# Stick-breaking attention on one core: moving a group's first exponential, the read-outs and the restored halves

## The chip, the core and the metric

The kernel runs on one core of a Trainium2 chip. The core has five engines that run their own instruction streams and meet at semaphores: TensorE (PE, with its weight loads shown apart as PEld), VectorE (DVE), ScalarE (ACT), GpSimd (POOL) and SyncE (SP), which here only issues DMAs. The metric is the device time of one execution in microseconds. The kernel before took 1867.29 us (median of three runs, 1866.61 to 1867.33).

## The reference, cut to what matters

Two decoder layers on 512 tokens of width 2048. The first is an indexer-sparse attention layer and isn't touched. The second is stick-breaking attention over shared keys and values, 16 query heads in 4 groups, each with one key and value head:

```python
def mixer_b(x, w_in, w_o, k, v):
    q, gate = jnp.split(x @ w_in, [WIDTH_B], axis=-1)
    ...
        z = jnp.einsum('bqngd,bsnd->bngqs', qg, k).astype(jnp.float32) * (HEAD_DIM ** -0.5)
        strict = key_pos[None, :] < t[:, None]
        log_om = jnp.where(strict, -jax.nn.softplus(z), 0.0)
        suffix = lax.cumsum(log_om, axis=log_om.ndim - 1, reverse=True) - log_om
        a = jnp.where(strict, jnp.exp(jax.nn.log_sigmoid(z) + suffix), 0.0)
        o = jnp.einsum('bngqs,bsnd->bqngd', a.astype(v.dtype), v)
    ...
    return (o * jax.nn.silu(gate)) @ w_o
```

Everything is in float32. The kernel reaches that precision by splitting each operand into a high part and the rest (`split`: ACT copies the high part, DVE subtracts) and multiplying three times (`mm3`).

## The kernel before, in words

Activations are kept transposed: a block is 128 features by 512 tokens, `XH[k]` and `XL[k]` are the high and low part of block k of the layer's input, k from 0 to 15. The change lies in one stretch of the program, the stick-breaking layer's attention, from the first logits to the output projection.

**Groups and units.** The stretch runs four groups, g = 0 to 3, of four heads each. In a group, PE works on two things in turns. One is the gate projection: 16 blocks of weights by 4 banks, 64 steps of three 512-column matmuls (`gate(n)` issues n steps; names `g`, `xh`, `xl`, `wh`, `wl`). The other is ten units, `Sticks.units`, each one a pair of query block i and key block kb, four heads by 128 queries wide. Units 0, 1, 5 and 8 are on the diagonal and get a mask. A unit passes these stages:

- `logits`: three matmuls into a PSUM bank `z` (unit 0 in bank 7, the others by turns in 4 and 5); on the diagonal DVE adds the mask.
- `soft` and `plus`: three ACT operations (Abs, Exp, Ln) and one DVE operation make the softplus.
- `high` and `low`: DVE adds the running total, casts the high part `sh` and subtracts the low part `sl`; for kb > 0 ACT copies the rows that carry the total out of z into `t`.
- `weights`: two matmuls with a triangle add the suffix sums onto the same bank z, ACT takes the exponential, and for kb > 0 DVE subtracts z from `t`. Only then is the bank free for the unit after next.
- `halves`: ACT and DVE split the result into two `c` tiles.
- `values`: three matmuls into a bank `o` (6 or 7). The third one multiplies the low half.
- `leave`: for kb = 0, ACT reads the finished bank o out into F (`f<-o`).

**Turns.** `turn(s, gaps)` for s = 1 to 11 holds the logits and softplus of unit s, the weights and halves of unit s - 1 and the values of unit s - 2, with gate steps between them (`gaps`, from `TURNS`: 54 steps in all). A turn is called late when unit s is on the diagonal. On PE, ACT and DVE the order of the instructions in this stretch is written out by hand: `strictly` issues each one after the one before on its engine. So an instruction that waits holds up whatever stands behind it on the same engine. GpSimd is called directly, without that order.

**Weights of the gate.** `feed(most, ahead)` pushes as many gate items as will be needed within `ahead` gate steps; each item is one ACT copy (`wh<-raw`) and one DVE subtraction (`wl<-raw,wh`) into three rotating buffers. The raw weights come by DMA of 512 KB into three `raw` buffers, in the order of the list `units`. `others(n)` takes n pieces off a background list `bg`, in which queries and keys of the next group and the restored halves wait.

**Restored halves.** The Strassen products before this stretch have overwritten the right half (256 columns) of blocks 0 to 7. They are read back from a scratch tensor `x2` in DRAM, four blocks with each of two 512 KB units, and `restore` splits them into XH and XL again. Group 0 takes the gate's blocks in the order 8 to 15, 0 to 7 (`gate_first`), so block 0 is needed from gate step 32.

**Start and end of a group.** Group 0 runs 11 gate steps before its first turn, the others 10. `first_soft` takes units 0 and 1 through soft, plus, high and low. At the end the gate's 64 steps are filled up, the next group's two logits follow, then `close` applies the SiLU of the gate banks, and the table of ACT is switched.

Of the kernel before, what the change touches and what calls it, by code (L numbers as in the profile page):

```python
# [10 lines left out]
F32 = mybir.dt.float32  # L11
# [3 lines left out]
ALU = mybir.AluOpType  # L15
# [3 lines left out]
T = 512  # L19
H = T // 2  # L20
D = 2048
NK = D // 128
# [55 lines left out]
def trunk_kernel(  # L78
# [48 lines left out]
    act, dve, pool = (Paced(e) for e in (nc.scalar, nc.vector, nc.gpsimd))  # L127
    pool = nc.gpsimd
# [11 lines left out]
    def split(hi, lo, src, eng=dve):  # L140
        act.activation(hi, src, AF.Copy)
        eng.tensor_tensor(lo, src, hi.bitcast(F32), ALU.subtract)
# [12 lines left out]
    XH = [top.tile([128, T], F32R, name=f"xh{k}") for k in range(NK)]  # L155
    XL = [top.tile([128, T], F32R, name=f"xl{k}") for k in range(NK)]
# [16 lines left out]
    units = []  # L173
# [14 lines left out]
    def next_raw():  # L188
        while sent[0] < len(units) and len(raws) < 3:
            raw = top.tile([128, 2, 512], F32, name="raw", tag="raw", bufs=3)  # L190
            unit = units[sent[0]]
            if len(unit) == 1:
                _, k, n = unit[0].shape
            else:
                k, n = 2, unit[-1]
            raw = raw.rearrange("p a n -> p (a n)")[:, : k * n].rearrange("p (k n) -> p k n", k=k)
            if len(unit) == 1:
                nc.sync.dma_start(raw, unit[0])
            else:
                src, a, b, c0, n = unit  # L200
                rows = src.rearrange("(k p) n -> p k n", p=128)
                step = b - a
                if sent[0] < 2:

                    for i, cut in enumerate(((0, H if sent[0] else NSEL, T), (0, T))):
                        for lo, hi in zip(cut, cut[1:]):
                            halves.append((raw[:, i, lo:hi], rows[:, a + i * step, c0 + lo : c0 + hi]))
                    if len(halves) == 6:
                        for n in (1, 3, 4, 2, 5, 0):
                            nc.sync.dma_start(*halves[n])  # L210
                else:
                    nc.sync.dma_start(raw, rows[:, a : b + 1 : step, c0 : c0 + n])
            raws.append(raw)
            sent[0] += 1
        return raws.popleft()
# [38 lines left out]
    def weight_parts():  # L254
        return tuple(top.tile([128, 512], F32R, name=n, tag=n, bufs=3) for n in ("wh", "wl"))

    def plain_items(jobs):
        for n, nk in jobs:
            if n <= 128:
                for k in range(0, nk, 4):  # L260
                    if k % 8 == 0:
                        raw = next_raw()
                    parts = weight_parts()
                    four = [w[:, : 4 * n].rearrange("p (k n) -> p k n", k=4) for w in parts]
                    split(*four, raw[:, k % 8 : k % 8 + 4])
                    yield from zip(*([w[:, a] for a in range(4)] for w in four))
                continue
            for _ in range(nk // 2):
                raw = next_raw()
                for a in range(2):  # L270
                    wh, wl = weight_parts()
                    split(wh[:, :n], wl[:, :n], raw[:, a])
                    yield wh, wl
# [81 lines left out]
    def strictly(fn, *args):  # L355
        was, pinned[0] = pinned[0], 2
        fn(*args)
        pinned[0] = was
# [212 lines left out]
    for g in range(4):  # L571
        add_job(w_in_b, g * 512, strassen=True)
    x2 = dram.tile([D, T], F32, name="x2")
    for k in (4, 5, 6, None, 7, 0, None, 1, 2, 3):
        if k is None:
            first = 4 * (units[-1][1] == 0)
            units.append((x2.rearrange("(k p) t -> p k t", p=128)[:, first : first + 4, H:T],))
        else:
            units.append((w_in_b, 2 * k, 2 * k + 1, D, 512))
# [69 lines left out]
    late = slice(NSEL, T)  # L649
# [526 lines left out]


    def restore(raw, k):
        split(XH[k][:, H:T], XL[k][:, H:T], raw[:, k % 4])

    def gate_items():
        for k, n in ((0, 6), (4, 4)):
            yield from plain_items([(512, n)])
            raw = next_raw()
            bg.extend(lambda raw=raw, k=k: restore(raw, k) for k in range(k, k + 4))
            if k:
                bg.append(lambda: split_keys(1))
        yield from plain_items([(512, 6), *[(512, NK)] * 3])

    C3.extend(c3_tiles(pc_.enter_context(tc.tile_pool(name="pc1", bufs=1))))  # L1190
    V, K = ([tuple(spots[n : n + 2]) for n in where] for where in ((0, 2, 4, 6), (8, 14) * 2))
# [2 lines left out]
    def split_keys(g):  # L1194
        split(*K[g], Kf[:, g])
# [4 lines left out]
    def split_scaled(g, i):  # L1200
        qh, ql = (q.rearrange("p (h q) -> p h q", h=4) for q in Q[i])
        src = F[g][:, :, i * 128 : (i + 1) * 128]
        act.activation(qh, src, AF.Copy, scale=HSCALE)
        dve.scalar_tensor_tensor(ql, src, HSCALE, qh.bitcast(F32), ALU.mult, ALU.subtract)
# [63 lines left out]
    class Sticks:  # L1268
# [3 lines left out]
        units = [(3, 3), (1, 1), (3, 2), (1, 0), (3, 1), (2, 2), (3, 0), (2, 1), (0, 0), (2, 0)]  # L1272
# [97 lines left out]
        def turn(self, s, gaps):  # L1370

            late = self.diagonal(s)
            new = 1 < s < 10
            if new:
                strictly(self.logits, s)
                if late:
                    strictly(self.low, s - 1)
                strictly(self.soft, s)
                if not late:
                    strictly(self.plus, s)  # L1380
                    feed(1)
            gate(gaps[0])
            if s > 1:
                strictly(self.values, s - 2)
            gate(gaps[1])
            if s < 11:
                strictly(self.weights, s - 1)
                if new and late:
                    strictly(self.plus, s)
                strictly(self.halves, s - 1)  # L1390
                if new:
                    strictly(self.high, s)
                    if not self.diagonal(s + 1):
                        strictly(self.low, s)
            else:
                strictly(act.preload_act_table_set, "silu_and_others")
            if s > 1:
                strictly(self.leave, s - 2)

            if self.g < 3:  # L1400
                bg.extend(lambda i=i: split_scaled(self.g + 1, i) for i in {8 if self.g == 0 else 6: (1,), 9: (3,), 10: (0,)}.get(s, ()))
            if new and late:
                feed(1)
            else:
                feed()
                others(1 if self.g else 2)
            gate(gaps[2])
# [3 lines left out]
    def gate(n):  # L1411
        steps(gemm, n)
        gated[0] += n

    def feed(most=9, ahead=10):

        while most and items.count < min(64, -(-(gated[0] + ahead) // 4)):
            strictly(items.push)
            most -= 1
# [2 lines left out]
        for _ in range(min(n, len(bg))):  # L1422
            strictly(bg.popleft())

    def first_soft(u, ahead=18):
        strictly(sticks.soft, u)
        strictly(sticks.plus, u)
        feed(1, ahead)
        strictly(sticks.high, u)
        strictly(sticks.low, u)  # L1430

    LOG_EXP = "natural_log_exp_and_others"
    tc.keep_in_program_order(act.preload_act_table_set(LOG_EXP))
# [3 lines left out]
    sticks = Sticks(0)  # L1437
    strictly(sticks.logits, 0)
    for u, n in enumerate((6, 5)):
        for _ in range(n):  # L1440
            gate(1)
            if not u:
                feed()
        if not u:
            strictly(sticks.logits, 1)
            first_soft(0)
            first_soft(1, 14)
    bg.append(lambda: split_scaled(0, 0))

    TURNS = ((0, 0, 3), *[(1, 1, 3)] * 3, (2, 1, 3), *[(1, 1, 3)] * 2, (2, 1, 3), (1, 1, 3), (1, 1, 2), (1, 1, 3))  # L1450
    for g in range(4):
        for s in range(1, 12):
            if g and s == 2:
                bg.append(lambda g=g: split_scaled(g, 2))
            if 0 < g < 3 and s == 3:
                bg.append(lambda g=g: split_keys(g + 1))
            sticks.turn(s, TURNS[s - 1])
        gate(64 * (g + 1) - gated[0])
        others(len(bg))
        if g < 3:  # L1460
            then = Sticks(g + 1)
            for u in range(2):
                strictly(then.logits, u)

        def close(h):
            sg = work()
            act.activation(sg, banks[h], AF.Silu)
            dve.tensor_tensor(F[g][:, h], F[g][:, h], sg, ALU.mult)

        for h in range(4):  # L1470
            strictly(close, h)
        if g < 3:
            sticks = then
            feed(1)
            strictly(act.preload_act_table_set, LOG_EXP)
            for u in range(2):
                first_soft(u)
            banks = mm_banks("g")
            gemm = gemm_w(items, plain, banks)
            gate(10)  # L1480
    pk_.close()
    pc_.close()

# [55 lines left out]
```

## Time and profile before

| what | value |
| --- | --- |
| median of three runs | 1867.29 us |
| profiled execution: device time | 1867.0 us |
| profiled execution: span, first to last instruction | 1865.3 us |
| granted TensorE clock, mean | 0.999 |
| PE busy / PEld busy | 99% / 84% of the span |
| DVE, ACT, POOL busy | 66%, 50%, under 1% |

In the rows, PE is the matmul and PEld the load of its stationary operand. A matmul's duration includes the pipeline behind it: 512-column matmuls are listed with 389 ns, though on an undisturbed stretch they start every 0.227 us. So a busy share of 99% doesn't mean that PE runs at its peak; lost time shows as a larger distance between two starts. The names are those of the program with their numbers left out: `x` in a DMA row is `x2`. L116 and L118 are lines of the helpers that issue ACT's and DVE's instructions, so instructions are told apart by their tiles.

### The profile page before, as it was taken

To read this page: it belongs to the slowest core of one execution; us is meant where nothing else is said; L and a number is where in the kernel's file an instruction comes from. 1 tells how busy PE (TensorE), PEld (TensorE's weight loads), DVE (VectorE), ACT (ScalarE), POOL (GpSimd) and SP (SyncE) were. 2 spreads that over 40 slices of the span, in tenths; PEclk is the share of its full clock that TensorE was granted. 3 is DMA by queue.
4 is the path that set the end of the run, shared out by engine and by line. 5 is a ranking of instruction groups with operands and counts; after the bars stand their busy time and mean duration, and the time that the engine had idled before them with its cause. 6 is when DMAs were issued, how large, how long until landed. Compare 5 with 4: busy or idle time off the path is not lost.

```text
span 1865.3 us, 24806 instructions
## 1 busy us (share of the span) xinstructions
PE 1855.9 (99%) x9181; PEld 1575.5 (84%) x9181; DVE 1231.2 (66%) x2395; ACT 939.0 (50%) x1696; POOL 4.7 (0%) x20
## 2 busy tenths in 40 slices
PE   9999999999999999999999999999999999999998
PEld 8898888888888888888888999987787888888887
DVE  5668678566556444676467788887878745567534
ACT  3546333355555432475245444478888743347422
POOL 0000000000000000000000000000000000000000
PEclk9999999999999999999999999999999999999999
DMA  6442333322221432433334333332122253243333
GB/s 198 128 116 66 98 95 97 96 68 69 68 69 57 158 120 78 125 97 106 126 118 127 110 93 109 107 90 81 57 69 78 69 187 95 76 128 97 118 102 113
DMA packets 111178, 189.21 MB, mean 101 GB/s; under 512 B 8528, under 2 KB 29008, under 8 KB 111056
## 3 DMA queue, kind: packets, MB, share of 16 engines
q1 hardware_dynamic: 111056, 187.62, 33.2%
q8 instruction: 72, 1.18, 0.3%
q14 instruction: 50, 0.41, 0.1%
HBM read 179.21 MB, written 8.39 MB: 101 GB/s over the span
## 4 chain that ended last, share of the span: by engine, by line
PE 93%; ACT 3%; DVE 2%; issue 1%; DMA 0%; SPq 0%; DVEq 0%; ACTq 0%
PE g L145 11%; PE g L147 11%; PE g L146 11%; PE o L147 7%; PE o L146 7%; PE o L145 7%; PE m L145 4%; PE m L147 4%; PE m L146 4%; PE q L145 3%; PE q L147 3%; PE q L146 3%; ACT wk L116 2%; PE k L146 2%; PE k L147 2%; PE k L145 2%
## 5 line engine op out<-in xcount | busy, mean ns | idle before, releaser
L118 ACT ACTIVATE wh<-raw 128x512 fp32r<-128x512 f32 (+2 forms) x624 | 359.5, 577 | 687.2 <-PE g L146 220.3
L118 DVE TENSOR_TENSOR wl<-raw,wh 128x512 fp32r<-128x512 f32 (+2 forms) x623 | 387.6, 623 | 438.2 <-ACT wh L118 423.4
L145 PE MATMUL g<-xh,wh 128*128 128x512 f32 x1024 | 403.6, 394 | 0.0
L147 PE MATMUL g<-xh,wl 128*128 128x512 f32 x1024 | 399.7, 390 | 0.2 <-DVE wl L116 0.2
L146 PE MATMUL g<-xl,wh 128*128 128x512 f32 x1024 | 399.3, 390 | 0.0
L147 PEld LDWEIGHTS g<-xh,wl 128*128 128x128 f32 x1024 | 192.2, 188 | 42.0 <-DVE wl L116 1.0
L146 PEld LDWEIGHTS g<-xl,wh 128*128 128x128 f32 x1024 | 192.5, 188 | 37.1
L145 PEld LDWEIGHTS g<-xh,wh 128*128 128x128 f32 x1024 | 192.4, 188 | 37.0
L147 PE MATMUL o<-xh,wl 128*128 128x512 f32 x512 | 199.3, 389 | 0.0
L145 PE MATMUL o<-xh,wh 128*128 128x512 f32 x512 | 199.2, 389 | 0.0
L146 PE MATMUL o<-xl,wh 128*128 128x512 f32 x512 | 199.2, 389 | 0.0
L147 PEld LDWEIGHTS o<-xh,wl 128*128 128x128 f32 x512 | 96.1, 188 | 20.4 <-DVE wl L118 0.4
L145 PEld LDWEIGHTS o<-xh,wh 128*128 128x128 f32 x512 | 96.1, 188 | 20.0
L146 PEld LDWEIGHTS o<-xl,wh 128*128 128x128 f32 x512 | 96.1, 188 | 19.9
L145 PE MATMUL q<-xh,wh 128*128 128x512 f32 x256 | 99.6, 389 | 0.0
L146 PE MATMUL q<-xl,wh 128*128 128x512 f32 x256 | 99.6, 389 | 0.0
L147 PE MATMUL q<-xh,wl 128*128 128x512 f32 x256 | 99.6, 389 | 0.0
L118 ACT ACTIVATE sh<-st 128x512 fp32r<-128x512 f32 x80 | 49.7, 624 | 44.2 <-DVE st L118 44.1
L116 ACT ACTIVATE wk<-z 128x512 f32<-128x512 f32 x80 | 47.6, 595 | 36.1 <-DVE z L116 14.6
L118 DVE TENSOR_TENSOR sl<-st,sh 128x512 fp32r<-128x512 f32 x80 | 55.1, 690 | 13.9 <-ACT sh L118 13.9
L118 DVE TENSOR_TENSOR xl<-f,xh 128x512 fp32r<-128x512 f32 x80 | 54.3, 686 | 12.5 <-ACT f L118 12.3
L147 PEld LDWEIGHTS q<-xh,wl 128*128 128x128 f32 x256 | 48.0, 188 | 10.1
(298 smaller groups left out, 3396.7 us busy)
## 6 DMA issues: line engine op xcount, KB each, us to landing
raw<-w_in_a SPq DMA_DIRECT2D x95, 512.0 KB, 3.7
raw<-w_in_b SPq DMA_DIRECT2D x64, 512.0 KB, 3.8
raw<-w_ple_gate SPq DMA_DIRECT2D x52, 512.0 KB, 3.7
raw<-w_o_a SPq DMA_DIRECT2D x24, 512.0 KB, 3.8
raw<-w_o_b SPq DMA_DIRECT2D x24, 512.0 KB, 3.7
raw<-w_kv_b SPq DMA_DIRECT2D x16, 512.0 KB, 3.8
raw<-w_ple_gate SPq DMA_DIRECT2D x24, 256.0 KB, 2.9
f<-xT SPq DMA_DIRECT2D x4, 1024.0 KB, 6.4
```

The source lines that it names most:

```text
L116: ins = method(*args, **kw)
L118: ins = method(*args, **kw)
L145: pe.matmul(out, a[0], b[0], start=start, stop=False)
L146: pe.matmul(out, a[0], b[1], start=False, stop=False)
L147: pe.matmul(out, a[1], b[0], start=False, stop=stop)
```

## The change

Four things are changed, all in that stretch.

1. `first_soft` becomes `first_two`: unit 0 goes through soft, plus, one gate item, high and low as before, unit 1 only through soft and plus. Its high and low move into turn 1, behind the exponential and the halves of unit 0 and behind one gate item. Turn 1 takes no background piece any more.
2. The gate runs 11 steps ahead of turn 1 in groups 1 to 3 too. The count at the end of a group stays 64, so one step fewer stands at the end.
3. In late turns the gate item is pushed ahead of `high` in place of behind the read-out. The read-outs of units 3 and 6 move from turns 5 and 8, which are late, to the ends of turns 6 and 9; those of units 8 and 9 stay.
4. `restore` no longer uses ACT: DVE copies the high half and GpSimd subtracts. The second 512 KB of x2 is loaded one unit earlier, ahead of the weights of blocks 0 and 1, which take its later place.

```diff
-    for k in (4, 5, 6, None, 7, 0, None, 1, 2, 3):
+    for k in (4, 5, 6, None, 7, None, 0, 1, 2, 3):
         if k is None:
-            first = 4 * (units[-1][1] == 0)
+            first = 4 * (units[-1][1] == 14)
             units.append((x2.rearrange("(k p) t -> p k t", p=128)[:, first : first + 4, H:T],))
...
     def restore(raw, k):
-        split(XH[k][:, H:T], XL[k][:, H:T], raw[:, k % 4])
+        hi, lo = XH[k][:, H:T], XL[k][:, H:T]
+        dve.tensor_copy(hi, raw[:, k % 4])
+        pool.tensor_tensor(lo, raw[:, k % 4], hi.bitcast(F32), ALU.subtract)
...
-        for k, n in ((0, 6), (4, 4)):
+        for k, n in ((0, 6), (4, 2)):
...
-        yield from plain_items([(512, 6), *[(512, NK)] * 3])
+        yield from plain_items([(512, 8), *[(512, NK)] * 3])
...
                 strictly(self.halves, s - 1)
-                if new:
+                if late or s == 1:
+                    feed(1)
+                if s < 10:
                     strictly(self.high, s)
                     if not self.diagonal(s + 1):
                         strictly(self.low, s)
             else:
                 strictly(act.preload_act_table_set, "silu_and_others")
-            if s > 1:
-                strictly(self.leave, s - 2)
...
-            if new and late:
-                feed(1)
-            else:
+            if not late:
+                for u in {6: (3,), 9: (6,), 10: (8,), 11: (9,)}.get(s, ()):
+                    strictly(self.leave, u)
                 feed()
                 others(1 if self.g else 2)
...
-    def first_soft(u, ahead=18):
-        strictly(sticks.soft, u)
-        strictly(sticks.plus, u)
-        feed(1, ahead)
-        strictly(sticks.high, u)
-        strictly(sticks.low, u)
+    def first_two():
+        for u in range(2):
+            strictly(sticks.soft, u)
+            strictly(sticks.plus, u)
+            if not u:
+                feed(1, 18)
+                strictly(sticks.high, u)
+                strictly(sticks.low, u)
...
-            first_soft(0)
-            first_soft(1, 14)
+            first_two()
...
-            for u in range(2):
-                first_soft(u)
+            first_two()
...
-            gate(10)
+            gate(11)
```

## The prediction

> **What bounds the kernel now.** I read the engines' busy times first, then the four groups as windows, each from its first logits to the next group's, and then the matmuls of an undisturbed stretch (name, count, duration, first and last start).
>
> ```profile
> PE 1855.9 (99%) x9181; PEld 1575.5 (84%) x9181; DVE 1231.2 (66%) x2395; ACT 939.0 (50%) x1696; POOL 4.7 (0%) x20
> ```
>
> ```profile
> 1234.03:1299.02 64.99, 63.91 (x275) 50.15 (x273) 53.14 (x91) 50.30 (x90) 1.24 (x6) 1.00 0.28 81
> 1299.02:1362.26 63.24, 62.65 (x272) 50.85 (x273) 49.73 (x82) 51.98 (x89) 0.00 (x0) 1.00 0.23 67
> 1362.26:1424.99 62.73, 62.27 (x273) 50.82 (x272) 49.89 (x82) 51.50 (x88) 0.00 (x0) 1.00 0.23 68
> 1424.99:1488.96 63.97, 63.08 (x273) 50.66 (x272) 49.92 (x81) 51.64 (x88) 0.00 (x0) 1.00 0.21 66
> ```
>
> ```profile
> L145 PE MATMUL o<-xh,wh x83: 389/389/389, 1489.0 to 1544.7; 128*128 128x512 f32 x83
> ```
>
> PE is the bound, and no matmul is removed. Undisturbed, 82 triples start in 55.7 us: 0.2264 us a matmul. A group is 64 x 3 + 10 x 8 = 272 matmuls, so 61.6 us. The four windows are longer by 3.4, 1.6, 1.1 and 2.4 us. These 8.5 us are all that the change can win, 0.45% of the time, and less than it can lose. So the question is which waits of PE go and which come. The list of PE's waits (total, times, longest) names the largest:
>
> ```profile
> PE o L1362 <- DVE c L116: 1.1, 3, 0.5
> PE z L145 <- DVE t L116: 1.0, 4, 0.4
> PE z L145 <- ACT f L116: 0.5, 1, 0.5
> ```
>
> It counts only time in which the modelled pipeline is empty. Starts in the timeline (start, duration) tell more:
>
> ```profile
> 1311.63 0.39 PE L1361 MATMUL o<-c,c 128*128 128x512 f32 x1
> 1312.39 0.50 PE L1362 MATMUL o<-c,c 128*128 128x512 f32 x1 [0.37 <-DVE c L116]
> 1312.73 0.39 PE L145 MATMUL g<-xh,wh 128*128 128x512 f32 x1
> ```
>
> The two distances, 0.76 and 0.34, exceed 0.227 by 0.53 and 0.11: 0.64 us where 0.37 is listed. I add 0.27 to each listed wait.
>
> **The change part by part.** *(a) The first exponential.* The wait above is unit 0's third values matmul, in group 1. Its way through ACT, and the start on DVE:
>
> ```profile
> 1307.21 1.30 ACT L116 ACTIVATE wk<-wk 128x512 f32<-128x512 f32 x2
> 1308.41 0.62 ACT L116 ACTIVATE wh<-raw 128x512 fp32r<-128x512 f32 x1
> 1309.26 0.59 ACT L116 ACTIVATE t<-z 32x512 f32<-32x512 f32 x1 [0.23 <-DVE wk L116]
> 1309.88 0.60 ACT L116 ACTIVATE wk<-z 128x512 f32<-128x512 f32 x1
> ...
> 1308.54 0.69 DVE L116 SCALAR_TENSOR_TENSOR wk<-z,wk 128x512 f32<-128x512 f32 x1 [0.95 <-ACT wk L116]
> ```
>
> The exponential (1309.88) stands behind unit 1's gate item and total. Moved up it starts at 1308.5, 1.4 us sooner, and the low half behind it comes at about 1311.0 in place of 1312.34. PE wants it at 1311.63 + 0.23 = 1311.86. All three waits of that kind go: 1.1 + 3 x 0.27 = 1.9 us. Late next is unit 1: its cast and low part now follow, on DVE, the softplus of 1308.54, the total, the half and a gate item. At 0.6 us each (steps between starts, as on ACT) that is 1308.54 + 4 x 0.6 + 0.45 + 0.69 = 1312.1; its weights want it one values matmul, one gate step and one matmul after 1311.86, at 1313.0. Margin 0.9 us. Small waits beside these, at the weights and values of the first units, I put at -0.3 (bounds 0 and -1).
>
> *(b) Eleven steps.* In groups 1 to 3 the step taken from the end stands at the start, so between unit 9's weights and the next unit 0's there are as many steps as before; only the logits in between come 0.68 us (three matmuls) sooner. Unit 0's bank is 7, which unit 9's read-out frees:
>
> ```profile
> 1359.80 1.28 ACT L116 ACT_TABLE_LOAD   x1
> 1361.10 0.60 ACT L116 ACTIVATE f<-o 128x512 f32<-128x512 f32 x1
> ...
> 1362.26 0.39 PE L145 MATMUL z<-c 128*128 128x512 f32 x1
> ...
> 1295.91 1.14 ACT L116 ACTIVATE c<-f 128x512 fp32r<-128x512 f32 x2
> 1298.37 0.60 ACT L116 ACTIVATE f<-o 128x512 f32<-128x512 f32 x1
> ...
> 1299.02 0.50 PE L145 MATMUL z<-c,c 128*128 128x512 f32 x1 [0.49 <-ACT f L116]
> ```
>
> At the first transition PE waits now: 0.49 + 0.27 = 0.76 us, and starts 0.65 us after the read-out starts. At the second PE wants the bank at 1362.26 - 0.68 = 1361.58 and gets it at 1361.10 + 0.65 = 1361.75: a new wait of 0.17 + 0.11 = 0.28 us, and the same at the third: +0.55. At the first, group 0 already ran 11 steps. There its background list is worked off one piece sooner (13 pieces, without turn 1's slots, but with x2's second part two items earlier), so the turn before the table load has one `c<-f` in place of the two of 1295.91: ACT is 0.52 ahead. -0.5 (bounds 0 and -0.76).
>
> *(c) Late turns.* Unit 7's logits wait for the total of unit 5, whose bank they take:
>
> ```profile
> 1332.49 0.59 ACT L116 ACTIVATE t<-z 1x512 f32<-1x512 f32 x1 [0.82 <-DVE wk L116]
> 1332.98 0.57 ACT L116 ACTIVATE f<-o 128x512 f32<-128x512 f32 x1
> 1333.46 0.62 ACT L116 ACTIVATE wh<-raw 128x512 fp32r<-128x512 f32 x1
> 1333.98 0.57 ACT L116 ACTIVATE wk<-z 128x512 f32<-128x512 f32 x1
> ...
> 1336.31 0.58 ACT L116 ACTIVATE wk<-z 128x512 f32<-128x512 f32 x1
> ...
> 1337.23 0.39 PE L147 MATMUL g<-xh,wl 128*128 128x512 f32 x1
> 1337.84 0.50 PE L145 MATMUL z<-c 128*128 128x512 f32 x1 [0.22 <-DVE t L116]
> ```
>
> The read-out (1332.98) and the gate item (1333.46) hold up unit 6's softplus, that one unit 5's exponential (1336.31), and that the total. Moved, the item fills the idle 0.82 us ahead of 1332.49 and the read-out is gone; ACT is 0.85 us sooner at the softplus and at least 0.6 at the exponential. The wait is 1337.84 - 1337.23 - 0.23 = 0.38, with its follower 0.49 us. It goes in groups 1 to 3: -1.5, and its smaller twin in group 0: -0.2. The read-out, later, is late for nobody: the next use of its bank is a turn away. What is inserted ahead of `high` puts 0.6 us of DVE before unit 5's low part; I take that as covered, at a cost of 0 to 0.3 a group. In group 0 items pushed late in turns 5 and 8 stop the gate itself:
>
> ```profile
> 1287.47 0.39 PE L146 MATMUL g<-xl,wh 128*128 128x512 f32 x1
> 1288.05 0.50 PE L147 MATMUL g<-xh,wl 128*128 128x512 f32 x1 [0.20 <-DVE wl L116]
> 1288.39 0.40 PE L1338 MATMUL z<-sh,tri 128*128 128x512 f32 x1
> ```
>
> 0.35 + 0.11 us in turn 8, and about 0.2 in turn 5. Pushed ahead of `high` they come 0.6 us or more sooner: -0.65.
>
> *(d) GpSimd.* No two-input operation on GpSimd stands in the trace. Rows by line, and what the restored halves cost DVE and ACT now (min, median, max ns; first and last start):
>
> ```profile
> L1266 POOL TENSOR_SCALAR_AFFINE_SELECT gone<-gone 128x128 f32<-128x128 f32 x2 | 0.5, 298 | 0.0
> L116 DVE TENSOR_TENSOR xl<-raw,xh x8: 416/418/420, 1254.2 to 1280.8; 128x256 fp32r<-128x256 f32 x8
> L116 ACT ACTIVATE xh<-raw x8: 397/402/418, 1251.6 to 1279.5; 128x256 fp32r<-128x256 f32 x8
> ```
>
> One subtraction of 256 columns lies between 0.3 us (that row) and 1.2 (twice the columns, two inputs). I take 0.7. It starts 14 us ahead of use (the first at 1254; block 0 is used from step 32, half of the group later), so its length is hidden. ACT loses 8 x 0.40 us, DVE's subtractions become copies of at most the same length: cost 0, bounds -0.5 and, if the two engines get in each other's way for 1.2 us in each of five turns, of which 0.4 reaches PE, +2. I take +0.3. [...]
>
> *(e) The DMA order.* x2's second part had this slot and is early now; the weights of blocks 0 and 1 get it:
>
> ```profile
> 1256.29 0.37 SPq L198 DMA_DIRECT2D raw<-x  x1
> DMA to landing us min/median/max: 3.5/3.7/4.0
> 1259.75 0.61 ACT L116 ACTIVATE wh<-raw 128x512 fp32r<-128x512 f32 x1
> ...
> 1271.72 0.61 ACT L116 ACTIVATE wh<-raw 128x512 fp32r<-128x512 f32 x1
> ```
>
> They land at 1256.29 + 3.7 = 1260.0; ACT wants them at 1259.75. It stops for 0.3 us, and with it unit 3's exponential, which waits for PE at that point anyway: 0, bound +0.5.
>
> Sum: -1.9 - 0.3 + 0.55 - 0.5 - 1.5 - 0.2 - 0.65 + 0.3 = **-4.2 us**. From the profiled 1867.0 us (span 1865.3 and 1.7 around it) that is 1862.8; the median of the runs is 0.3 higher, so **1863.1 us**.
>
> **The rivals.** *The waits move to the next unit.* The margins of 0.9 us in (a) and of one turn in (c) are sums of six or seven steps. If each group's chain is a microsecond longer, PE waits about 0.4 at unit 1's weights or unit 3's logits, four times: 1863.1 + 1.6 = 1864.7. For it: DVE now has five operations in a row there. Against: PE-paced steps in between leave the engines time to catch up. *GpSimd costs DVE its slack* in group 0, where the four windows show DVE busiest (53.14 us): the bound of (d), or a long first operation, gives back 2 to 4 us: 1866. [...] *GpSimd is much slower than I take it.* x2's first part holds a raw buffer until its fourth subtraction; the weights that follow into it are wanted by ACT at 1271.72, so the buffer must be free at 1268.0. From 1254.2 on, four in a row have 13.8 us: from 3.45 us each ACT and then PE wait, and from 4.5 us each (4.2 us late) the kernel is slower than before. At 6 us each: 10 us late, 1873. Against it: the 298 ns row. *All of it goes*, the small waits of group 0 included, and no lock: 1867.3 - 6.5 = 1860.8.
>
> **How the numbers follow.** Forecast 0.55 (1861.7 to 1864.6), waits move 0.19, GpSimd takes slack 0.10, GpSimd slow 0.05, all goes 0.11. The range 1860.6 to 1866.8 leaves out the slow case and little of the others. About 0.2%, 3.7 us, is what a measurement of this kernel can tell from no change; the forecast passes 1863.56 by 0.5. So faster: 0.6 of the first, all of the last and a little of the second, 0.49; slower: 0.06; same: 0.45.
>
> **What would show it.** Right: in the profile after, the waits of `o` L1362 on `c` and of `z` on `t` in groups 1 to 3 gone; the first exponential of a group directly behind the second softplus; windows near 63.8, 62.2, 62.0 and 62.5 us with the new wait of `z` on `f<-o` at the second and third transition. Wrong: waits of `z` on `sl` in the second unit, GpSimd rows over 1.2 us with DVE operations of two inputs lengthened beside them, or ACT stopped at a `wh<-raw` for a DMA near 1260 or 1272.

## The result, and the profile after

The changed kernel takes 1863.18 us (median of 14 runs, 1862.78 to 1863.92), the kernel before 1866.95 us (14 runs, 1866.60 to 1867.48): 3.8 us less, ratio 0.998 with a 95% interval of 0.9972 to 0.9988. The two sets of runs don't overlap. The span of the profiled execution went from 1865.3 to 1861.9 us.

By its busy times and its list of PE's waits the changed kernel hardly waits any more. First the busy times of the whole execution, then the only line of that list that lies in the stretch:

```profile
PE 1854.8 (100%) x9181; PEld 1576.4 (85%) x9181; DVE 1230.9 (66%) x2395; ACT 937.7 (50%) x1688; POOL 11.8 (1%) x28
```

```profile
PE z L145 <- DVE t L116: 0.2, 1, 0.2
```

The three waits of `o` on `c` and the one of `z` on `f<-o` are gone from it, and of four waits of `z` on `t` one is left. The list of the weight loads still has smaller ones, 2.7 us in five waits of `z` on `t` where PE's has 0.2 us in one (waiting engine and line, releaser, total us, times, longest):

```profile
PEld z L145 <- DVE t L116: 2.7, 5, 0.7
PEld z L1340 <- DVE sl L116: 2.3, 7, 0.5
...
PEld z L145 <- ACT f L116: 1.2, 3, 0.4
```

The four groups as windows, from the first logits of one to those of the next, as before (bounds, length, then busy us and instructions of PE, PEld, DVE, ACT, POOL):

```profile
1234.32:1297.56 63.24, 62.99 (x274) 50.42 (x272) 52.86 (x91) 48.17 (x82) 8.38 (x14) 1.00 0.27 84
1297.56:1360.13 62.57, 62.45 (x273) 50.82 (x272) 49.70 (x81) 51.77 (x88) 0.00 (x0) 1.00 0.22 68
1360.13:1422.72 62.59, 62.46 (x273) 50.83 (x272) 49.72 (x81) 51.78 (x88) 0.00 (x0) 1.00 0.23 68
1422.72:1485.56 62.84, 62.62 (x274) 50.94 (x273) 49.28 (x80) 51.57 (x88) 0.00 (x0) 1.00 0.22 68
```

They are shorter by 1.75, 0.67, 0.14 and 1.13 us, 3.7 us together. The forecast had 63.8, 62.2, 62.0 and 62.5: group 0 gained more than that, the others less.

The first exponential stands where the change puts it. ACT in group 1 (start, duration):

```profile
1305.75 1.30 ACT L116 ACTIVATE wk<-wk 128x512 f32<-128x512 f32 x2
1307.21 0.60 ACT L116 ACTIVATE wk<-z 128x512 f32<-128x512 f32 x1 [0.16 <-PE z L1340]
1307.84 0.63 ACT L116 ACTIVATE c<-wk 128x512 fp32r<-128x512 f32 x1
```

It waits 0.16 us for PE's matmuls and for nothing else. But a wait has appeared that the forecast doesn't have. PE, the weight load of its second row, and then DVE, in turns 3 and 4 of group 1:

```profile
1319.25 0.39 PE L147 MATMUL g<-xh,wl 128*128 128x512 f32 x1
1319.76 0.50 PE L145 MATMUL z<-c,c 128*128 128x512 f32 x1
1320.09 0.39 PE L146 MATMUL z<-c,c 128*128 128x512 f32 x1
...
1319.76 0.19 PEld L145 LDWEIGHTS z<-c,c 128*128 128x128 f32 x1 [0.54 <-DVE t L116]
...
1317.83 0.69 DVE L116 SCALAR_TENSOR_TENSOR wk<-z,wk 128x512 f32<-128x512 f32 x1
1318.44 0.68 DVE L116 TENSOR_TENSOR wl<-raw,wh 128x512 fp32r<-128x512 f32 x1
1319.04 0.67 DVE L116 TENSOR_TENSOR t<-t,z 1x512 f32<-1x512 f32 x1
```

Unit 4's logits start 0.51 us after the matmul ahead of them, and the next one 0.33 us later: 0.28 + 0.11 = 0.39 us lost. They wait for the bank of unit 2, which the DVE operation of 1319.04 frees, and a gate item (`wl`, 1318.44) stands ahead of it. No `[... <-]` stands behind the matmul's row, only 0.12 us lie between the listed end of the one ahead (1319.64) and its start; the distance of the starts and the weight load show it. The same happens in groups 2 and 3: 1.2 us in all.

### The profile page after: what moved, and what is told of

Same layout as the page of the kernel before. It is cut to its first block, busy times and chain, and to the rows that moved or that the text cites. A ratio compares the mean times of both kernels' runs of the same rounds, so it can differ in the third digit from the quotient of the medians.

```text
span 1861.9 us, 24820 instructions
## 1 busy us (share of the span) xinstructions
PE 1854.8 (100%) x9181; PEld 1576.4 (85%) x9181; DVE 1230.9 (66%) x2395; ACT 937.7 (50%) x1688; POOL 11.8 (1%) x28
## 4 chain that ended last, share of the span: by engine, by line
PE 97%; DVE 2%; ACT 1%; issue 0%; DMA 0%; SPq 0%
PE g L145 12%; PE g L147 12%; PE g L146 12%; PE o L147 7%; PE o L145 7%; PE o L146 7%; PE m L145 4%; PE m L147 4%; PE m L146 4%; PE q L147 3%; PE q L145 3%; PE q L146 3%; PE k L146 2%; PE k L147 2%; PE k L145 2%; PE iq L147 1%
## 5 line engine op out<-in xcount | busy, mean ns | idle before, releaser
L146 PEld LDWEIGHTS q<-xl,wh 128*128 128x128 f32 x256 | 48.0, 188 | 10.1
```

Source lines behind the costliest of these rows:

```text
L146: pe.matmul(out, a[0], b[1], start=False, stop=False)
```

## The experiments

All twelve kernels were timed beside the kernel before, whose median lay between 1866.76 and 1866.95 us in every comparison. Differences below are those of medians; where the sets of runs overlap, it is said. In the fourteen profiles the first logits of group 0 start between 1233.57 and 1234.41 us, though the program ahead of them is the same. So a few tenths between two medians can come from outside the stretch; where they matter, the length of the stretch in the profile is given too, from the first logits to the first matmul of the output projection. It is 251.24 us in the changed kernel.

### One part undone at a time

**The first exponential.** Unit 1's gate item, high and low go ahead of it again:

```diff
-            if not u:
-                feed(1, 18)
-                strictly(sticks.high, u)
-                strictly(sticks.low, u)
+            feed(1, 14 if u and not sticks.g else 18)
+            strictly(sticks.high, u)
+            strictly(sticks.low, u)
...
-                if s < 10:
+                if new:
                     strictly(self.high, s)
```

> The changed kernel with part (a) undone alone: unit 1's gate item, high and low stand again ahead of the group's first exponential; eleven steps, late turns, read-outs and GpSimd stay as changed. Theory (the exponential's place removed the waits of unit 0's third values matmul): these waits come back in groups 1 to 3, 0.64 + 0.51 + 0.74 = 1.9 us; the new waits of unit 4's logits in groups 1 to 3 (0.39 us each) go, because DVE gets the freed time back: net +0.7 us, 1863.9. Rival (the waits only moved to unit 4, the part is worth nothing): 1863.2. Rival (its worth is the whole 1.9 and the unit 4 waits come from elsewhere): 1865.1.

1864.25 us (1863.77 to 1864.85), 1.1 us slower than the changed kernel, nearest to the theory. The wait of unit 0's third values matmul is back, most of it in group 3. PE there:

```profile
1436.27 0.40 PE L1363 MATMUL o<-c,c 128*128 128x512 f32 x1
1437.08 0.50 PE L1364 MATMUL o<-c,c 128*128 128x512 f32 x1 [0.41 <-DVE c L116]
1437.41 0.40 PE L145 MATMUL g<-xh,wh 128*128 128x512 f32 x1
```

0.58 + 0.11 us here, but only 0.2 and 0.1 in groups 1 and 2, and the wait of unit 4's logits shrank from 0.39 to about 0.24 and didn't go. About 1.0 us of waits came back and 0.5 went. So the theory had the place and the direction; the second half of it, that this part had made the new wait, holds for 0.15 of these 0.39 us.

**The eleventh step.**

```diff
-            gate(11)
+            gate(10)
```

> The changed kernel with gate(10) in place of gate(11) in groups 1 to 3, the rest as changed. Theory (the step only moves): the waits for bank 7 at the second and third transition go (2 x 0.25 us), and at unit 0's weights 0.1 to 0.5 us come back in groups 1 and 3: between -0.5 and +0.3 us, 1863.1. Rival (the step of lead is what pays): each of three groups loses about the 0.4 us by which the step outruns the new wait, +1.2 us, 1864.4.

1861.51 us (1861.29 to 1861.83): 1.7 us **faster** than the changed kernel, outside of both expectations. The waits for bank 7 at the second and third transition are gone, as the theory says, and at unit 0's weights 0.2 and 0.8 us are there in groups 1 and 3, where the changed kernel loses nothing and 0.35: the places are the theory's, the sum of 0.65 us is a little over its 0.5. But the 1.2 us of unit 4's logits are gone too. DVE and PE at that place in group 1:

```profile
1316.74 0.69 DVE L116 SCALAR_TENSOR_TENSOR wk<-z,wk 128x512 f32<-128x512 f32 x1
1317.35 0.66 DVE L116 TENSOR_TENSOR t<-t,z 1x512 f32<-1x512 f32 x1
...
1318.15 0.39 PE L147 MATMUL g<-xh,wl 128*128 128x512 f32 x1
1318.38 0.39 PE L145 MATMUL z<-c,c 128*128 128x512 f32 x1
```

The gate item between the softplus and the total isn't there. `feed` pushes items until their number reaches (steps done + 10) / 4, rounded up. At the start of turn 3 a group has done 18 steps with the lead of ten and 19 with eleven: 28 / 4 = 7 items, 29 / 4 rounds up to 8. The step that was to give the first unit time also moved an item ahead of unit 2's total.

**Late turns and read-outs.**

```diff
-                if late or s == 1:
+                if s == 1:
                     feed(1)
...
+            if s > 1:
+                strictly(self.leave, s - 2)
...
-            if not late:
-                for u in {6: (3,), 9: (6,), 10: (8,), 11: (9,)}.get(s, ()):
-                    strictly(self.leave, u)
+            if new and late:
+                feed(1)
+            elif not late:
                 feed()
```

> The changed kernel with part (c) undone alone: in late turns the gate item is pushed behind high again, the read-outs of units 3 and 6 stand in turns 5 and 8 again. Theory: the waits of unit 7's logits come back in groups 1 to 3 (0.49 us each) and group 0's waits for gate weights and for unit 7 (0.9 us): +2.4 us, 1865.6. Rival (only the earlier gate item matters, or these waits were gone for another reason): +0.9 us or less, 1864.1 or less.

1866.66 us (1866.09 to 1867.27): 3.5 us slower, most of the whole gain, and more than expected. The weight loads of this kernel:

```profile
PEld z L145 <- DVE t L116: 4.3, 9, 0.7
PEld g L147 <- DVE wl L116: 3.0, 8, 0.6
```

Unit 7's logits wait again, 0.23 us a group. The gate's own weights wait eight times; in the kernel before it was twice, in group 0, the only one with eleven steps. Now PE loses some 0.3 us at them in each of groups 1 to 3 as well. So part of these 3.5 us is the price of eleven steps without the earlier items; ten steps without them weren't tried.

**GpSimd.**

```diff
-        hi, lo = XH[k][:, H:T], XL[k][:, H:T]
-        dve.tensor_copy(hi, raw[:, k % 4])
-        pool.tensor_tensor(lo, raw[:, k % 4], hi.bitcast(F32), ALU.subtract)
+        split(XH[k][:, H:T], XL[k][:, H:T], raw[:, k % 4])
```

> The changed kernel with restore as before (ACT copies, DVE subtracts; x2's parts still loaded in the new order). Theory of the prediction (the move costs 0.3 us for the time in which DVE is locked out, and ACT's eight copies were hidden): -0.3 us, 1862.9, between -0.6 and +0.3. Rival (taking 3.2 us off ACT and 1.1 us off DVE pays): +0.5 us or more, 1863.7, with group 0's window alone longer.

1863.41 us (1862.96 to 1864.24): 0.2 us slower, with runs that overlap. The sign is the rival's, the size neither's. The stretch takes 251.27 us against 251.24, so its profile shows no difference either way.

### What made the new wait

**Items nine steps ahead.** Eleven steps stay; in groups 1 to 3 `feed` counts one step less:

```diff
-    def feed(most=9, ahead=10):
+    def feed(most=9, ahead=None):
+        ahead = ahead or (9 if sticks.g else 10)
```

> The changed kernel, eleven steps kept, but the gate items of groups 1 to 3 are pushed 9 steps ahead in place of 10, so that a whole item falls where it fell with ten steps: the item at the start of turn 3 moves to that turn's end, behind the total of unit 2. Theory A (the eleventh step lifts feed's count over a multiple of four, and the extra gate item ahead of unit 2's total on DVE makes unit 4's logits wait): these waits go in three groups, 3 x 0.39 = 1.2 us, and nothing else changes: 1862.0. Theory B (the waits come from the later place of the weights against the logits, so from the step itself): 1863.2 as the changed kernel.

1861.73 us (1861.55 to 1862.41), 1.45 us faster. In the starts of PE's matmuls no wait at unit 4's logits is left in these groups; the list of weight loads has `z` on `t` 1.1 us in 2 waits, where the changed kernel has 2.7 in 5. Theory A holds: the wait came with the item that the rounding put ahead of the total.

**The read-out ahead of the table load.**

```diff
             else:
+                strictly(self.leave, 9)
                 strictly(act.preload_act_table_set, "silu_and_others")
...
-                for u in {6: (3,), 9: (6,), 10: (8,), 11: (9,)}.get(s, ()):
+                for u in {6: (3,), 9: (6,), 10: (8,)}.get(s, ()):
```

> The changed kernel, with the last read-out of a group (unit 9, bank 7) ahead of ACT's table load in turn 11 in place of behind it. Theory (the next group's first logits wait for bank 7 behind the table load, 0.24 to 0.25 us at each of three transitions): all three waits go, 0.1 to 0.25 us of it comes back at unit 0's weights in group 3, which PE reaches sooner: -0.5 us, 1862.7. Rival (the waits are those of another bank or of the masks): 1863.2.

1862.59 us (1862.31 to 1863.13), 0.6 us faster. ACT at the second transition, where the table load of 1.28 us now stands behind the read-out:

```profile
1357.18 0.60 ACT L116 ACTIVATE f<-o 128x512 f32<-128x512 f32 x1
1357.79 1.28 ACT L116 ACT_TABLE_LOAD   x1
1359.09 0.63 ACT L116 ACTIVATE wh<-raw 128x512 fp32r<-128x512 f32 x1
```

No wait of `z` on `f<-o` is left in its list. As expected a part came back at unit 0's weights in group 3, where PE now loses 0.72 us in place of 0.36.

**Both edits together.**

> Both edits at once: items of groups 1 to 3 pushed 9 steps ahead, last read-out ahead of the table load. If both theories hold and the two don't touch: 1.2 + 0.5 = 1.7 us under the changed kernel, 1861.5, as ten steps gave. If either only moves a wait: 1862.3 or more.

1861.39 us (1861.26 to 1862.05). They nearly add up: 1.8 of 1.45 + 0.59.

**Ten steps and the read-out.** `gate(10)`, ten ahead, read-out ahead of the load:

> Ten steps in groups 1 to 3, items pushed 10 ahead as in the kernel before, and the last read-out ahead of the table load. Theory (with the waits for bank 7 gone and the items at their old places, an eleventh step has nothing left to give or take but a few tenths at unit 0's weights): 1861.3, as with eleven steps, nine ahead and the read-out moved (1861.4). Rival (eleven steps pay once their two side effects are gone): 1862.0 or more.

1861.42 us (1861.32 to 1861.62), as with eleven. With its two side effects gone, the eleventh step has no worth that the time shows. The starts show what it trades: with ten steps PE loses 0.51 and 0.79 us at unit 0's weights in groups 1 and 3, with eleven 0.71 us in group 3 alone and 0.1 us behind unit 9's weights in each of groups 1 to 3.

### GpSimd and the DMA at their limits

**Every subtraction three times.**

```diff
-        pool.tensor_tensor(lo, raw[:, k % 4], hi.bitcast(F32), ALU.subtract)
+        for _ in range(3):
+            pool.tensor_tensor(lo, raw[:, k % 4], hi.bitcast(F32), ALU.subtract)
```

> The changed kernel, with each of GpSimd's eight subtractions issued three times (same result): 16 more of 0.75 us. Theory (GpSimd and DVE's two-input operations shut each other out, 0.3 us of one operation showed it): DVE operations beside them grow by up to 2 us, group 0's waits grow by 1 to 3 us: 1865. Rival (what GpSimd does is hidden, the one long DVE row is chance): 1863.2.

1869.47 us (1868.23 to 1870.41): 6.3 us slower, twice the most that the theory allowed. First the changed kernel: GpSimd's subtractions (min, median, max ns), and one place where DVE met them.

```profile
L1181 POOL TENSOR_TENSOR xl<-raw,xh x8: 735/744/1222, 1254.9 to 1280.2; 128x256 fp32r<-128x256 f32 x8
...
1259.63 1.44 POOL L1181 TENSOR_TENSOR xl<-raw,xh 128x256 fp32r<-128x256 f32 x2 [3.99 <-DVE xh L116]
...
1260.62 1.00 DVE L116 TENSOR_TENSOR wl<-raw,wh 128x512 fp32r<-128x512 f32 x1
```

`wl` takes 0.68 us elsewhere; here 1.00: it starts while GpSimd is at its second subtraction, and ends 0.55 us after that has ended. The longest subtraction took 1222 ns. With three times as many, many of DVE's rows beside them grow, though not all (a `wl` at 1260.69 took its usual 0.69 us), and PE waits for them:

```profile
1260.05 10.59 POOL L1182 TENSOR_TENSOR xl<-raw,xh 128x256 fp32r<-128x256 f32 x12 [2.03 <-DVE xh L116]
...
1262.46 1.22 DVE L116 TENSOR_TENSOR wk<-wk,t 1x512 f32<-1x512 f32 x1
1263.71 0.85 DVE L116 CAST sh<-wk 128x512 fp32r<-128x512 f32 x1
1264.48 1.57 DVE L116 CAST xh<-raw 128x256 fp32r<-128x256 f32 x2
...
1286.87 0.50 PE L1341 MATMUL z<-sl,down 128*128 128x512 f32 x1 [2.04 <-DVE sl L116]
```

0.67, 0.43 and 0.49 us are what these DVE rows take in the changed kernel (1262.38 to 1263.92), where GpSimd stands idle until 1263.79. GpSimd's own 24 subtractions took 957 ns in the mean (907 in the changed kernel, where the shortest took 735). So the two engines do hold each other up, and at eight subtractions there was room for it. The theory names DVE's operations with two inputs; in this trace the casts grew too, from 0.43 to 0.85 us and from 0.49 to 1.57. Waits of 1.4 and 2.2 us at low parts are most of the loss, and a fall of PE's clock behind the second, shown at the end, is about 1.5 us of it.

**Nine steps ahead in group 0 too.**

```diff
-    def feed(most=9, ahead=10):
+    def feed(most=9, ahead=9):
```

> The changed kernel with items pushed 9 steps ahead in all four groups, group 0 too. In group 0 the item at the start of turn 3 goes behind unit 2's total as in the others, but its DVE subtraction is what frees the raw buffer for the weights of blocks 0 and 1, whose DMA so starts about 1.5 us later, near 1257.5, and lands near 1261.2, while ACT wants them near 1259.5. Theory: group 0 loses its 0.5 us wait of unit 4's logits and gets 0.5 to 1.5 us of waits behind the late item: 1861.7 to 1862.7. Rival (the new place of x2's second part costs nothing even then): 1861.2.

1866.03 us (1865.30 to 1867.36): 2.9 us slower than the changed kernel, and 4.3 us slower than with nine steps in groups 1 to 3 alone, which is what the edit costs in group 0. The theory had the mechanism, and its size far too small. First the changed kernel's ACT, then this kernel's SP, ACT and PE:

```profile
1259.96 0.63 ACT L116 ACTIVATE wh<-raw 128x512 fp32r<-128x512 f32 x1 [0.20 <-DMA raw<-w_in_b]
```

```profile
1259.59 26.19 SPq L212 DMA_DIRECT2D raw<-w_in_b  x5
...
1263.34 0.63 ACT L116 ACTIVATE wh<-raw 128x512 fp32r<-128x512 f32 x1 [4.11 <-DMA raw<-w_in_b]
...
1264.50 0.50 PE L145 MATMUL z<-c,c 128*128 128x512 f32 x1 [2.68 <-ACT wk L116]
```

The DVE subtraction that frees the buffer slid behind a whole `high` and `low`, to 1258.88, so the DMA went out at 1259.59, 3.4 us later than in the changed kernel. ACT stood for 4.1 us. One position in DVE's order turned a wait of 0.2 us into one of 4.1.

### The last wait, and what is left for GpSimd

**Blocks 0 and 1 placed by hand.** On top of both edits, with the two splits for the output projection left out of `finish_layer` for this layer:

```diff
+            if g == 3 and s in (4, 7):
+                bg.append(lambda k=s // 7: split(*plain(k), fblock(k)))
             sticks.turn(s, TURNS[s - 1])
```

> The last read-out ahead of the table load, items of groups 1 to 3 pushed 9 steps ahead, and besides: the splits of blocks 0 and 1 for the output projection, which fall by themselves between unit 0's softplus and its high part in group 3 (two operations on ACT, two on DVE), are placed in turns 4 and 7 of group 3. Theory (they hold up unit 0's low part, for which PE waits 0.61 + 0.11 us at unit 0's weights in group 3): this wait goes, and nothing else: 0.7 us under the kernel with the first two edits, 1860.7. Rival (the wait is ACT's table load and feed, as in the groups before): 1861.4.

1860.35 us (1860.24 to 1860.70): 1.0 us faster than without (the stretch is 0.9 us shorter, where 0.7 was expected), 6.5 us faster than the kernel before (ratio 0.9965, 0.9953 to 0.9978). ACT in group 3 of the kernel without, where two foreign `xh<-f` stand in unit 0's softplus and behind it:

```profile
1425.86 0.60 ACT L116 ACTIVATE wk<-z 128x512 f32<-128x512 f32 x1
1426.36 0.62 ACT L118 ACTIVATE xh<-f 128x512 fp32r<-128x512 f32 x1
1426.88 1.29 ACT L116 ACTIVATE wk<-wk 128x512 f32<-128x512 f32 x2
1428.07 0.62 ACT L116 ACTIVATE wh<-raw 128x512 fp32r<-128x512 f32 x1
1428.59 0.62 ACT L118 ACTIVATE xh<-f 128x512 fp32r<-128x512 f32 x1
```

The order by hand fixes what stands behind what among its own instructions; others may still be put between. Unit 0's weights no longer wait in group 3.

**The same without GpSimd.** `restore` as in the kernel before:

> The kernel with blocks 0 and 1 in turns 4 and 7, nine steps and the read-out ahead of the table load (1860.35), with restore back on ACT and DVE. If moving the subtractions to GpSimd is worth nothing either way, as its undoing in the changed kernel could not tell (+0.2): 1860.2 to 1860.6. If GpSimd's locking out of DVE costs what the prediction put it at: 1860.0. If ACT's 3.2 us were worth something: 1860.8 or more.

1860.79 us (1860.11 to 1861.15): 0.4 us slower, the runs overlap. Twice the undoing came out slower, by 0.2 and 0.4. But the stretch takes 248.71 us here and 248.75 with GpSimd; in the pair above it was 251.27 and 251.24. In both pairs of profiles it is as long with GpSimd as without it to a few hundredths, so the tenths between the medians aren't shown to come from the move.

## Why the prediction was right, and where it was not

The kernel is 3.8 us faster than the kernel before, where the sum had 4.2. That 1863.18 lies so near 1863.1 is luck in part: the forecast stood on a median of three runs that is 0.3 us above that of the 14, and its terms missed in both directions. The waits below are read off the starts in the two traces.

- **(a) The exponential.** The three waits of the values matmul are gone, 1.9 us as said, and unit 1's weights don't wait. Undone, only 1.0 us of these waits came back, 0.7 of it in group 3. That the eleventh step had taken away the rest in groups 1 and 2 is likely; it wasn't tried. For the small waits at the weights and values of the first units 0.3 us was taken, and 0.9 went.
- **(b) Eleven steps: the step that failed.** The waits for bank 7 came as worked out, 0.24 and 0.25 us where 0.28 was forecast, and at the first transition 0.25 of 0.75 us is left. What was wrong is "between unit 9's weights and the next unit 0's there are as many steps as before; only the logits in between come 0.68 us sooner". The number of steps is also what `feed` counts by, and one more put a gate item ahead of unit 2's total in three groups, 1.2 us. The term was +0.55; undoing the step gave 1.7 us. The rival "the waits move to the next unit" had the size of one wait (0.4 us) and a neighbouring place, but another reason: the chains that it names, at unit 1's weights and unit 3's logits, kept their margins.
- **(c) Late turns.** The waits of unit 7 and of the gate's items went, in all groups: 2.35 us forecast, 2.4 measured. That undoing it costs 3.5 us doesn't speak against the term, since with eleven steps the late items make PE wait in groups 1 to 3 too, where they didn't before.
- **(d) GpSimd.** One subtraction is 744 ns (0.7 taken). The two engines do hold each other up, which the prediction calls a lock: beside GpSimd two DVE rows of the changed kernel took 0.94 and 1.00 us in place of 0.69 and 0.68, and one subtraction took 1.22 us. But DVE had room for it: no run shows the 0.3 us of the sum, nor a gain, and the stretch takes 251.24 us with the move and 251.27 without it. The rival of a slow GpSimd set in at 3.45 us a block, by way of the raw buffer. With three subtractions a block, at least 2.2 us, the loss was there already, most of it by way of DVE. A small part came as that rival says: a DMA of weights that goes out at 1264.56 in the changed kernel went out at 1269.97, ACT stopped for 0.72 us, and PE lost 0.45.
- **(e) The DMA.** ACT stops for 0.20 us; 0.3 was forecast and called hidden, which it was.
- **The balance.** Too little was taken for (b), by 1.2 us, and PE now loses 0.1 us behind unit 9's weights in groups 1 to 3 as well. Against that stand 0.6 us more at the first units, and the 0.3 of (d) that wasn't spent. Which edit took away the small waits wasn't tried.

Two of the signs that were to show the prediction wrong did appear: a GpSimd row over 1.2 us (1222 ns) with DVE operations of two inputs lengthened beside GpSimd (0.94 and 1.00 us), and ACT stopped at a `wh<-raw` near 1260. PE's starts show no loss behind either.

## What to carry to other kernels

A lead that is counted in steps has a second reader if something else is paced by the same count: before adding a step, work out at which turns the rounding tips. In an order written by hand, ask of each moved instruction not only what waits for it but which buffer its end frees and which DMA stands behind that. And where an engine has waits of a few tenths at a dozen places, look at the distances between starts: the list of PE's waits showed 0.2 us in a stretch that still lost 4.8 (its four windows against 61.6 us each).

## What the hardware showed beside

After the long waits of PE in two kernels its granted clock fell, to 0.56 and 0.58 in the windows given here. In the kernel with nine steps everywhere, three windows around the wait (the column behind POOL is the granted clock):

```profile
1257.00:1264.50 7.50, 4.83 (x22) 3.62 (x20) 3.86 (x8) 3.00 (x6) 1.43 (x2) 1.00 0.21 70
1264.50:1268.16 3.66, 3.66 (x10) 2.83 (x11) 3.17 (x8) 1.43 (x3) 0.99 (x2) 0.56 0.00 0
1268.16:1272.00 3.84, 3.84 (x18) 3.21 (x17) 1.40 (x3) 3.34 (x6) 0.94 (x1) 0.97 0.43 137
```

From 1265.17 to 1268.16 matmuls started every 0.43 us in place of 0.227, and about 1.5 us were lost on top of the wait of 2.8. With GpSimd tripled the same followed a wait of 2.2 us (granted clock 0.58 from 1287.21 to 1291.31), and didn't follow one of 1.4 us (1.00 from 1267.30 to 1271.00). So in these two traces the waits of 2.2 and 2.8 us cost PE more than themselves. It seems not to happen in every execution: with GpSimd tripled, four of the eleven show a mean clock of 1.000 and take 1868.2 to 1868.7 us, the other seven 0.998 or 0.999 and 1869.5 to 1870.4.
